# Variance of rows: TensorE's row sums replaced by passes on DVE and ACT, with a new assignment of rows to partitions

## The chip, the cores and the metric

The kernel runs on one core of a Trainium2 chip. The metric is the time of one execution on the device in microseconds (us), taken as the median of several runs. The engines named below are TensorE (PE, the matrix engine), VectorE (DVE), ScalarE (ACT), GpSimd (POOL) and SyncE (SP), which here only issues DMA transfers. The core has 16 DMA engines, which move data between HBM and the on-chip memory.

## The reference

```python
def setup_inputs():
    batch, seq, dim = 32, 512, 1024
    return {"x": np.random.randn(batch, seq, dim).astype(np.float32)}

def reference(x):
    mean_sq = np.mean(x**2, axis=-1)
    sq_mean = np.mean(x, axis=-1)**2
    return (mean_sq - sq_mean).astype(np.float32)
```

For each of 32 x 512 = 16384 rows of 1024 float32 values, the variance is wanted: 67.1 MB are read and 64 KB written.

## The kernel before

**Layout.** The rows are spread over 128 partitions, 128 rows in a row for each partition. "Column" c is the set of the c-th rows of all partitions, so a load of n columns (`col_range`) takes n x 4 KB of contiguous memory for each partition, and the pitch from partition to partition is 128 rows, 512 KB.

**Loads.** SP issues all loads, in this order: `xt_fill` (columns 120 to 127, L79), then 13 groups of 8 columns (`xt`, L165) in a pool of three buffers, then the end columns 104 to 119 into `xt_end` (L195) in loads of 4, 4, 2, 2, 2, 1 and 1 columns. The load of group g+3 waits until group g's buffer is free; the loads of `xt_end` and `xt_fill` have memory of their own.

**Work on a group.** Each row needs its mean and its mean square. There are three ways:

- `do_bn_col`: DVE takes statistics of two halves of 512 elements (L112) and aggregates them to mean and variance (L115). Columns 0 to 2 of a group.
- `do_square_col` on ACT (L118) gives the mean square of columns 3 to 7. The sum of columns 3 and 4 is a reduction on DVE (L171).
- The sum of columns 5 to 7: `do_tensor_cols` transposes and adds eight blocks of 128 x 128 on TensorE (L133), DVE copies the result to `folded` (L142), and TensorE multiplies by a column of ones (L143).

In groups 2 to 9 one column of `xt_fill` is done beside, by ACT and TensorE. `combine` turns sums and mean squares into variances with a short Square on ACT (L83) and a subtraction on DVE (L90, L102). ACT issues the store of columns 0 to 103 (L189).

**End.** The 16 columns of `xt_end` go by the pattern "CSAA": C is ACT's mean square with DVE's reduction (L206), S is two passes on ACT (L118 and L213), A is `do_bn_col`. After the last column a Square on ACT (L221), a subtraction on DVE (L230) and the store of columns 104 to 127 on SP (L237) follow.

**Order.** Each engine runs its own list of instructions in order, and semaphores hold an instruction until its inputs are there. The framework places the semaphores and may move an instruction a little within its engine's list.

Of the kernel before, what the change touches and what calls it, by code (L numbers as in the profile page):

```python
# [3 lines left out]

# [4 lines left out]


# [1 line left out]
def kernel(  # L13
# [2 lines left out]
    x: bass.AP,  # L16
    out: bass.AP,
):
    nc = tc.nc
    P = nc.NUM_PARTITIONS  # L20
    FP32 = mybir.dt.float32

    xf = x.flatten_outer_dims()
    N, D = xf.shape
    assert N % P == 0
    ntiles = N // P
    DCH = D // P

    def col_range(c0, n):
        return dataclasses.replace(  # L30
            xf,
            offset=c0 * D,
            ap=[[ntiles * D, P], [D, n], [1, D]],
        )

    out_ji = dataclasses.replace(out, offset=0, ap=[[ntiles, P], [1, ntiles]])

    FMAX = nc.vector.BN_STATS_FMAX
    nsub = (D + FMAX - 1) // FMAX

    inv_sqrt_d = 1.0 / math.sqrt(D)

    NBODY = 13
    END0 = NBODY * 8
    FILL0 = 120

    end_plan = [
        (104, 4),
        (108, 4),
        (112, 2),  # L50
        (114, 2),
        (116, 2),
        (118, 1),
        (119, 1),
    ]

    xpool = ctx.enter_context(tc.tile_pool(name="xpool", bufs=3))
    spool = ctx.enter_context(tc.tile_pool(name="spool", bufs=8))
    fpool = ctx.enter_context(tc.tile_pool(name="fpool", bufs=4))
    scpool = ctx.enter_context(tc.tile_pool(name="scpool", bufs=2))  # L60
    opool = ctx.enter_context(tc.tile_pool(name="opool", bufs=1))
    ppool = ctx.enter_context(tc.tile_pool(name="ppool", bufs=5, space=bass.MemoryType.PSUM))
    pspool = ctx.enter_context(tc.tile_pool(name="pspool", bufs=2, space=bass.MemoryType.PSUM))

    ident = opool.tile([P, P], FP32)
    masks.make_identity(nc, ident)
    ones = opool.tile([P, 1], FP32)
    nc.gpsimd.memset(ones, 1.0)

    pair_stage = opool.tile([P, 2, ntiles], FP32)  # L70
    msq_stage = opool.tile([P, ntiles], FP32)
    sqm_stage = opool.tile([P, ntiles], FP32)

    scratch = scpool.tile([P, D], mybir.dt.bfloat16)

    xt_end = opool.tile([P, FILL0 - END0, D], FP32)
    xt_fill = opool.tile([P, ntiles - FILL0, D], FP32)

    nc.sync.dma_start(out=xt_fill, in_=col_range(FILL0, ntiles - FILL0))  # L79

    def combine(c0, ngrp, gsize, nbn):
        n = ngrp * gsize
        nc.scalar.activation(  # L83
            out=sqm_stage[:, c0 : c0 + n],
            in_=pair_stage[:, 0, c0 : c0 + n],
            func=mybir.ActivationFunctionType.Square,
            scale=1.0 / D,
        )
        if nbn == 0:
            nc.vector.tensor_tensor(  # L90
                out=pair_stage[:, 1, c0 : c0 + n],
                in0=msq_stage[:, c0 : c0 + n],
                in1=sqm_stage[:, c0 : c0 + n],
                op=mybir.AluOpType.subtract,
            )
        else:
            var_v = pair_stage[:, 1, c0 : c0 + n].rearrange(
                "p (g k) -> p g k", k=gsize
            )
            msq_v = msq_stage[:, c0 : c0 + n].rearrange("p (g k) -> p g k", k=gsize)  # L100
            sqm_v = sqm_stage[:, c0 : c0 + n].rearrange("p (g k) -> p g k", k=gsize)
            nc.vector.tensor_tensor(  # L102
                out=var_v[:, :, nbn:gsize],
                in0=msq_v[:, :, nbn:gsize],
                in1=sqm_v[:, :, nbn:gsize],
                op=mybir.AluOpType.subtract,
            )

    def do_bn_col(xcol, i):
        stats = spool.tile([P, nsub, 6], FP32, name="stats")  # L110
        for s in range(nsub):
            nc.vector.bn_stats(  # L112
                out=stats[:, s, :], in_=xcol[:, s * FMAX : (s + 1) * FMAX]
            )
        nc.vector.bn_aggr(out=pair_stage[:, :, i], in_=stats)  # L115

    def do_square_col(xcol, i):
        nc.scalar.activation(  # L118
            out=scratch,
            in_=xcol,  # L120
            func=mybir.ActivationFunctionType.Square,
            scale=inv_sqrt_d,
            accum_out=msq_stage[:, i : i + 1],
        )

    def do_tensor_cols(xt, cols):
        if not cols:
            return
        psum_s = pspool.tile([P, 8], FP32, name="psum_s")
        for slot, (k, i) in enumerate(cols):  # L130
            psum_f = ppool.tile([P, P], FP32, name="psum_f")
            for ch in range(DCH):
                nc.tensor.matmul(  # L133
                    out=psum_f,
                    lhsT=xt[:, k, ch * P : (ch + 1) * P],
                    rhs=ident,
                    is_transpose=True,
                    start=(ch == 0),
                    stop=(ch == DCH - 1),
                )  # L140
            folded = fpool.tile([P, P], FP32, name="folded")
            nc.vector.tensor_copy(out=folded, in_=psum_f)  # L142
            nc.tensor.matmul(  # L143
                out=psum_s[:, slot : slot + 1],
                lhsT=folded,
                rhs=ones,
                start=True,
                stop=True,
            )
        i0 = cols[0][1]  # L150
        nt = len(cols)
        nc.vector.tensor_copy(  # L152
            out=pair_stage[:, 0, i0 : i0 + nt], in_=psum_s[:, :nt]
        )

    def do_filler_col(j):
        i = FILL0 + j
        do_square_col(xt_fill[:, j, :], i)
        do_tensor_cols(xt_fill, [(j, i)])

    for gi in range(NBODY):
        c0 = gi * 8
        nbn, ncl = 3, 2
        xt = xpool.tile([P, 8, D], FP32, name="xt")
        nc.sync.dma_start(out=xt, in_=col_range(c0, 8))  # L165

        for k in range(nbn):
            do_bn_col(xt[:, k, :], c0 + k)
        for k in range(nbn, 8):
            do_square_col(xt[:, k, :], c0 + k)  # L170
        nc.vector.reduce_sum(  # L171
            out=pair_stage[:, 0, c0 + nbn : c0 + nbn + ncl],
            in_=xt[:, nbn : nbn + ncl, :],
            axis=mybir.AxisListType.X,
        )
        do_tensor_cols(
            xt, [(k, c0 + k) for k in range(nbn + ncl, 8)]
        )

        if 2 <= gi <= 9:  # L180
            do_filler_col(gi - 2)

        if gi == 7:
            combine(0, 8, 8, 3)
        elif gi == 10:
            combine(120, 1, 8, 0)
        elif gi == 12:
            combine(64, 5, 8, 3)
            nc.scalar.dma_start(  # L189
                out=out_ji[:, 0:END0], in_=pair_stage[:, 1, 0:END0]  # L190
            )

    for (c0, ncols) in end_plan:
        off = c0 - END0
        nc.sync.dma_start(  # L195
            out=xt_end[:, off : off + ncols, :], in_=col_range(c0, ncols)
        )
        for k in range(ncols):
            i = c0 + k
            mode = "CSAA"[(i - END0) % 4]  # L200
            xcol = xt_end[:, off + k, :]
            if mode == "A":
                do_bn_col(xcol, i)
            elif mode == "C":
                do_square_col(xcol, i)
                nc.vector.reduce_sum(  # L206
                    out=pair_stage[:, 0, i : i + 1],
                    in_=xcol,
                    axis=mybir.AxisListType.X,
                )  # L210
            else:
                do_square_col(xcol, i)
                nc.scalar.activation(  # L213
                    out=scratch,
                    in_=xcol,
                    func=mybir.ActivationFunctionType.Copy,
                    accum_out=pair_stage[:, 0, i : i + 1],
                )

    n_end = ntiles - END0  # L220
    nc.scalar.activation(  # L221
        out=sqm_stage[:, END0:ntiles],
        in_=pair_stage[:, 0, END0:ntiles],
        func=mybir.ActivationFunctionType.Square,
        scale=1.0 / D,
    )
    var_v = pair_stage[:, 1, END0:ntiles].rearrange("p (g k) -> p g k", k=4)
    msq_v = msq_stage[:, END0:ntiles].rearrange("p (g k) -> p g k", k=4)
    sqm_v = sqm_stage[:, END0:ntiles].rearrange("p (g k) -> p g k", k=4)
    nc.vector.tensor_tensor(  # L230
        out=var_v[:, :, 0:2],
        in0=msq_v[:, :, 0:2],
        in1=sqm_v[:, :, 0:2],
        op=mybir.AluOpType.subtract,
    )

    nc.sync.dma_start(  # L237
        out=out_ji[:, END0:ntiles], in_=pair_stage[:, 1, END0:ntiles]
    )


# [28 lines left out]
```

## Time and profile before

| | us |
|---|---|
| median of 3 runs | 167.70 (167.53 to 167.71) |
| profiled execution, first to last instruction (span; the page gives no other time for it) | 165.9 |
| DVE busy | 107.0 |
| ACT busy | 99.7 |
| TensorE matmul busy | 82.8 |
| mean rate of the DMA engines over the span | 405 GB/s |

The span runs from the first to the last instruction on the core. "Busy" is time in which an engine executed an instruction. Busy shares are means over the whole span; which engine or transfer sets the end is read from the waits and from the windows of each stage. A line number in a profile is a line of the kernel that the profile belongs to.

### The profile page before, as it was taken

Reading aid. Unit: us, or ns where it says so; the run is one execution under the profiler, and the core shown is the slowest. Engines: PE = TensorE matmul, PEld = TensorE weight load, DVE = VectorE, ACT = ScalarE, POOL = GpSimd, SP = SyncE. Lnnn points to the kernel's source line nnn. Section 1 sums busy time; section 2 is a strip of 40 time slices with the busy share of each in tenths; the row PEclk is TensorE's granted clock in tenths of the full one; section 3 lists DMA queues with packets and bytes.
Section 4 is the critical chain, followed back from the end, with each engine's and each line's share of the span. In section 5 each row is a group of like instructions: output and inputs, shape, how many; then the busy total and the mean of one; then the engine's idle time right before and its main releaser. Section 6 shows DMA issues by size and latency. Waiting matters only on the chain.

```text
span 165.9 us, 1460 instructions
## 1 busy us (share of the span) xinstructions
PE 82.8 (50%) x470; PEld 78.6 (47%) x470; DVE 107.0 (64%) x230; ACT 99.7 (60%) x175; POOL 0.7 (0%) x7
## 2 busy tenths in 40 slices
PE   0000047293791957749497774929565391950000
PEld 0000046292780947749396764829464381930000
DVE  0000049295791967949396794939769393999993
ACT  3000049093790967939396694939767391998981
POOL 1000000000000000000000000000000000000000
PEclk9999999658576597865858598795978658585555
DMA  5999999999999999999999999999999999999930
GB/s 190 443 427 450 411 450 411 443 443 427 450 399 450 421 435 435 421 443 411 443 423 443 427 435 435 419 450 415 435 435 419 443 421 399 435 417 417 412 140 3
DMA packets 3320, 67.26 MB, mean 405 GB/s; under 512 B 625, under 2 KB 625, under 8 KB 881
## 3 DMA queue, kind: packets, MB, share of 16 engines
q1 hardware_dynamic: 3168, 67.12, 94.7%
q8 instruction: 3, 0.05, 0.1%
q10 hardware_dynamic: 144, 0.05, 0.1%
q14 instruction: 5, 0.03, 0.1%
HBM read 67.11 MB, written 0.07 MB: 405 GB/s over the span
## 4 chain that ended last, share of the span: by engine, by line
DMA 69%; DVE 28%; issue 0%; SPq 0%; ACT 0%; ACTq 0%
DMA xt<-in_x_dram 69%; DVE stats L112 16%; DVE pair_stage L171 7%; DVE pair_stage L206 3%; DVE pair_stage L115 2%; DVE folded L142 0%; SPq L79 0%; ACT sqm_stage L221 0%; SPq L165 0%; DVE pair_stage L230 0%; DVE pair_stage L102 0%; DVE pair_stage L152 0%; ACTq L221 0%
## 5 line engine op out<-in xcount | busy, mean ns | idle before, releaser
L118 ACT ACTIVATE scratch<-xt 128x1024 bf16<-128x1024 f32 x65 | 68.7, 1057 | 59.6 <-DMA xt<-in_x_dram 57.9
L133 PE MATMUL psum_f<-ident,xt 128*128 128x128 f32 x312 | 62.9, 392 | 53.9 <-DMA xt<-in_x_dram 53.9
L133 PEld LDWEIGHTS psum_f<-ident,xt 128*128 128x128 f32 x312 | 59.1, 212 | 54.9 <-DMA xt<-in_x_dram 31.8
L112 DVE BATCH_NORM_STATS2 stats<-xt 128x6 f32<-128x512 f32 x78 | 48.8, 667 | 50.5 <-DMA xt<-in_x_dram 50.5
L171 DVE TENSOR_REDUCE pair_stage<-xt 128x2 f32<-128x2048 f32 x13 | 29.5, 2270 | 0.0
L143 PEld LDWEIGHTS psum_s<-ones,folded 128*128 128x128 f32 x94 | 11.5, 191 | 14.6 <-DVE folded L142 14.6
L143 PE MATMUL psum_s<-ones,folded 128*128 128x1 f32 x94 | 12.5, 252 | 11.4 <-DVE folded L142 11.4
L118 ACT ACTIVATION_READ_ACCUMULATOR scratch<-xt 128x1 f32 x65 | 12.1, 186 | 0.0
L112 DVE BATCH_NORM_STATS2 stats<-xt_end 128x6 f32<-128x512 f32 x16 | 10.1, 666 | 0.0
L142 DVE COPY folded<-psum_f 128x128 f32<-128x128 f32 x47 | 9.8, 267 | 0.0
L115 DVE BATCH_NORM_AGGREGATE pair_stage<-stats 128x2 f32<-128x12 f32 x47 | 9.2, 197 | 0.1
L118 ACT ACTIVATE scratch<-xt_end 128x1024 bf16<-128x1024 f32 x8 | 8.5, 1056 | 1.1 <-DMA xt_end<-in_x_dram 0.9
L133 PE MATMUL psum_f<-ident,xt_fill 128*128 128x128 f32 x64 | 9.0, 286 | 0.0
L118 ACT ACTIVATE scratch<-xt_fill 128x1024 bf16<-128x1024 f32 x8 | 8.5, 1057 | 0.3
L133 PEld LDWEIGHTS psum_f<-ident,xt_fill 128*128 128x128 f32 x64 | 8.2, 155 | 0.0
L152 DVE COPY pair_stage<-psum_s 128x3 f32<-128x3 f32 (+1 forms) x21 | 3.3, 159 | 5.2 <-PE psum_s L143 4.7
L206 DVE TENSOR_REDUCE pair_stage<-xt_end 128x1 f32<-128x1024 f32 x4 | 4.7, 1185 | 0.0
L213 ACT ACTIVATE scratch<-xt_end 128x1024 bf16<-128x1024 f32 x4 | 4.2, 1056 | 0.1
L118 ACT ACT_TABLE_LOAD x1 | 1.3, 1283 | 0.7 <-PEq L254 0.7
L118 ACT ACTIVATION_READ_ACCUMULATOR scratch<-xt_end 128x1 f32 x8 | 1.5, 186 | 0.0
L118 ACT ACTIVATION_READ_ACCUMULATOR scratch<-xt_fill 128x1 f32 x8 | 1.5, 186 | 0.0
L83 ACT ACTIVATE sqm_stage<-pair_stage 128x64 f32<-128x64 f32 (+2 forms) x3 | 0.7, 228 | 0.7 <-DVE pair_stage L152 0.7
(12 smaller groups left out, 2.7 us busy)
## 6 DMA issues: line engine op xcount, KB each, us to landing
xt<-in_x_dram SPq DMA_DIRECT2D x13, 4096.0 KB, 23.1
xt_fill<-in_x_dram SPq DMA_DIRECT2D x1, 4096.0 KB, 12.6
xt_end<-in_x_dram SPq DMA_DIRECT2D x2, 2048.0 KB, 29.8
xt_end<-in_x_dram SPq DMA_DIRECT2D x3, 1024.0 KB, 36.1
xt_end<-in_x_dram SPq DMA_DIRECT2D x2, 512.0 KB, 24.1
out_dram<-pair_stage ACTq DMA_DIRECT2D x1, 52.0 KB, 6.8
out_dram<-pair_stage SPq DMA_DIRECT2D x1, 12.0 KB, 1.4
```

The lines of the kernel that those rows point to most:

```text
L83: nc.scalar.activation(out=sqm_stage[:, c0 : c0 + n], in_=pair_stage[:, 0, c0 : c0 + n], func=mybir.ActivationFunctionType.Square, scale=1 ...
L112: nc.vector.bn_stats(out=stats[:, s, :], in_=xcol[:, s * FMAX : (s + 1) * FMAX])
L115: nc.vector.bn_aggr(out=pair_stage[:, :, i], in_=stats)
L118: nc.scalar.activation(out=scratch, in_=xcol, func=mybir.ActivationFunctionType.Square, scale=inv_sqrt_d, accum_out=msq_stage[:, i : i + 1],)
L133: nc.tensor.matmul(out=psum_f, lhsT=xt[:, k, ch * P : (ch + 1) * P], rhs=ident, is_transpose=True, start=(ch == 0), stop=(ch == DCH - 1),)
L142: nc.vector.tensor_copy(out=folded, in_=psum_f)
L143: nc.tensor.matmul(out=psum_s[:, slot : slot + 1], lhsT=folded, rhs=ones, start=True, stop=True,)
L152: nc.vector.tensor_copy(out=pair_stage[:, 0, i0 : i0 + nt], in_=psum_s[:, :nt])
L171: nc.vector.reduce_sum(out=pair_stage[:, 0, c0 + nbn : c0 + nbn + ncl], in_=xt[:, nbn : nbn + ncl, :], axis=mybir.AxisListType.X,)
L206: nc.vector.reduce_sum(out=pair_stage[:, 0, i : i + 1], in_=xcol, axis=mybir.AxisListType.X,)
L213: nc.scalar.activation(out=scratch, in_=xcol, func=mybir.ActivationFunctionType.Copy, accum_out=pair_stage[:, 0, i : i + 1],)
```

## The change

TensorE, GpSimd's constants, PSUM and the short subtractions at the end are no longer used. Every column is done by one engine alone: DVE by statistics and aggregation as before, ACT by a Copy pass that gives the negative mean (scaled by the root of 1/D) and a Square pass with that as its bias, whose accumulated output is the variance. In a group of 8, ACT takes columns 0, 3 and 6 and DVE the other five; ACT does its three Copy passes first and then its three Square passes.

There is no `xt_fill`. The 13 groups come first; 24 end columns follow in loads of 7, 5, 4, 2, 2, 1 and 1 columns, and columns 126 and 127 in two halves of 512 elements each, taken by DVE half by half. The first 127 columns have 127 rows in a row per partition (pitch 508 KB), and column 127 is the last 128 rows of the input, one per partition. Two stores end the kernel: ACT stores columns 0 to 126 (508 bytes per partition) once column 126 is done, and SP stores column 127 (4 bytes per partition).

```diff
-    def col_range(c0, n):
-        return dataclasses.replace(
-            xf, offset=c0 * D, ap=[[ntiles * D, P], [D, n], [1, D]],
-        )
+    MAIN = ncols - 1
+    def load(dst, c0, n, f0=0, f=D):
+        if c0 == MAIN:
+            offset, ap = MAIN * P * D, [[D, P], [1, f]]
+        else:
+            offset, ap = c0 * D, [[MAIN * D, P], [D, n], [1, f]]
+            if n == 1:
+                ap = [[MAIN * D, P], [1, f]]
+        nc.sync.dma_start(
+            out=dst, in_=dataclasses.replace(xf, offset=offset + f0, ap=ap)
+        )
...
-    end_plan = [(104, 4), (108, 4), (112, 2), (114, 2), (116, 2), (118, 1), (119, 1)]
+    END_LOADS = [7, 5, 4, 2, 2, 1, 1]
+    END_WHO = "ADDADDADADDADADDADDADA"
...
-    nc.sync.dma_start(out=xt_fill, in_=col_range(FILL0, ntiles - FILL0))
...
+    def dve_col(xcol, c):
+        stats = spool.tile([P, 2, 6], FP32, name="stats")
+        dve_half(stats, 0, xcol[:, :H])     # bn_stats
+        dve_half(stats, 1, xcol[:, H:])     # bn_stats
+        dve_done(stats, c)                  # bn_aggr into mv[:, :, c]
+
+    def act_cols(cols):
+        s = D ** -0.5
+        for xcol, c in cols:
+            nc.scalar.activation(out=junk, in_=xcol, func=ACTF.Copy,
+                scale=-s / D, accum_out=neg_mean[:, c : c + 1])
+        for xcol, c in cols:
+            nc.scalar.activation(out=junk, in_=xcol, func=ACTF.Square,
+                scale=s, bias=neg_mean[:, c : c + 1],
+                accum_out=mv[:, 1, c : c + 1])
...
+    for g in range(NGROUPS):
+        c0 = g * GROUP
+        xt = xpool.tile([P, GROUP, D], FP32, name="xt")
+        load(xt, c0, GROUP)
+        act_cols([(xt[:, k, :], c0 + k) for k in (0, 3, 6)])
+        for k in (1, 2, 4, 5, 7):
+            dve_col(xt[:, k, :], c0 + k)
...
+    for j in range(k, ncols - END0):
+        stats = spool.tile([P, 2, 6], FP32, name="stats")
+        for h in range(2):
+            xh = xt_end[:, j, h * H : (h + 1) * H]
+            load(xh, END0 + j, 1, h * H, H)
+            dve_half(stats, h, xh)
+        dve_done(stats, END0 + j)
+        if END0 + j == MAIN - 1:
+            nc.scalar.dma_start(
+                out=dataclasses.replace(out, offset=0, ap=[[MAIN, P], [1, MAIN]]),
+                in_=mv[:, 1, :MAIN],
+            )
+    nc.sync.dma_start(
+        out=dataclasses.replace(out, offset=MAIN * P, ap=[[1, P], [1, 1]]),
+        in_=mv[:, 1, MAIN:],
+    )
```

More of the change, by code (lines that the diff above doesn't have):

```diff
@@ L2 @@
 import dataclasses
-import math
 from contextlib import ExitStack
@@ L7 @@
 import concourse.tile as tile
-from concourse import bass_utils, masks, mybir
+from concourse import mybir
 from concourse._compat import with_exitstack
@@ L21 @@
     FP32 = mybir.dt.float32
+    ACTF = mybir.ActivationFunctionType
     xf = x.flatten_outer_dims()
@@ L25 @@
     assert N % P == 0
-    ntiles = N // P
-    DCH = D // P
-    def col_range(c0, n):
-        return dataclasses.replace(
-            xf,
-            offset=c0 * D,
-            ap=[[ntiles * D, P], [D, n], [1, D]],
-        )
[L36 to L55, printed above, removed]
+    ncols = N // P
@@ new lines @@
+    H = D // 2
+    MAIN = ncols - 1
[8 more added lines that the diff above has]
+            out=dst, in_=dataclasses.replace(xf, offset=offset + f0, ap=ap)
+        )
+    GROUP = 8
+    NGROUPS = 13
+    END0 = GROUP * NGROUPS
+    END_LOADS = [7, 5, 4, 2, 2, 1, 1]
@@ L57 @@
+    END_WHO = "ADDADDADADDADADDADDADA"
     xpool = ctx.enter_context(tc.tile_pool(name="xpool", bufs=3))
     spool = ctx.enter_context(tc.tile_pool(name="spool", bufs=8))
-    fpool = ctx.enter_context(tc.tile_pool(name="fpool", bufs=4))
-    scpool = ctx.enter_context(tc.tile_pool(name="scpool", bufs=2))
     opool = ctx.enter_context(tc.tile_pool(name="opool", bufs=1))
-    ppool = ctx.enter_context(tc.tile_pool(name="ppool", bufs=5, space=bass.MemoryType.PSUM))
-    pspool = ctx.enter_context(tc.tile_pool(name="pspool", bufs=2, space=bass.MemoryType.PSUM))
@@ L65 @@
[L65 to L77, printed above, removed]
-    nc.sync.dma_start(out=xt_fill, in_=col_range(FILL0, ntiles - FILL0))
@@ L81, in combine @@
[L81 to L87, printed above, removed]
-        )
[L89 to L94, printed above, removed]
-            )
-        else:
-            var_v = pair_stage[:, 1, c0 : c0 + n].rearrange(
-                "p (g k) -> p g k", k=gsize
-            )
[L100 to L235, printed above, removed]
+    mv = opool.tile([P, 2, ncols], FP32)
@@ new lines, with dve_half, dve_done @@
+    neg_mean = opool.tile([P, ncols], FP32)
+    junk = opool.tile([P, D], mybir.dt.bfloat16)
+    xt_end = opool.tile([P, ncols - END0, D], FP32)
+    def dve_half(stats, h, xh):
+        nc.vector.bn_stats(out=stats[:, h, :], in_=xh)
+    def dve_done(stats, c):
+        nc.vector.bn_aggr(out=mv[:, :, c], in_=stats)
+    def dve_col(xcol, c):
[3 more added lines that the diff above has]
+        dve_done(stats, c)
@@ new lines, in act_cols @@
+    def act_cols(cols):
+        s = D ** -0.5
+        for xcol, c in cols:
+            nc.scalar.activation(
+                out=junk,
+                in_=xcol,
+                func=ACTF.Copy,
+                scale=-s / D,
+                accum_out=neg_mean[:, c : c + 1],
+            )
+        for xcol, c in cols:
+            nc.scalar.activation(
+                out=junk,
+                in_=xcol,
+                func=ACTF.Square,
+                scale=s,
+                bias=neg_mean[:, c : c + 1],
+                accum_out=mv[:, 1, c : c + 1],
+            )
@@ new lines @@
+    for g in range(NGROUPS):
[5 more added lines that the diff above has]
+            dve_col(xt[:, k, :], c0 + k)
+    k = 0
+    for n in END_LOADS:
+        load(xt_end[:, k : k + n, :] if n > 1 else xt_end[:, k, :], END0 + k, n)
+        act_cols(
+            [
+                (xt_end[:, j, :], END0 + j)
+                for j in range(k, k + n)
+                if END_WHO[j] == "A"
+            ]
+        )
+        for j in range(k, k + n):
+            if END_WHO[j] == "D":
+                dve_col(xt_end[:, j, :], END0 + j)
+        k += n
@@ L237 @@
+    for j in range(k, ncols - END0):
[9 more added lines that the diff above has]
+                in_=mv[:, 1, :MAIN],
+            )
     nc.sync.dma_start(
-        out=out_ji[:, END0:ntiles], in_=pair_stage[:, 1, END0:ntiles]
+        out=dataclasses.replace(out, offset=MAIN * P, ap=[[1, P], [1, 1]]),
+        in_=mv[:, 1, MAIN:],
```

## The prediction

> **What bounds the kernel now.** I read the page's slices and queue table first, then the chain of waits in order of time, the windows by stage, and last the timeline of the end.
>
> ```profile
> span 165.9 us, 1460 instructions
> ...
> DMA  5999999999999999999999999999999999999930
> ...
> q8 instruction: 3, 0.05, 0.1%
> ...
> q14 instruction: 5, 0.03, 0.1%
> ```
>
> All 16 DMA engines are busy from the second slice to the 38th. So loading is the bound, and an engine matters only where it delays a load or stands behind the last one. The chain of waits gives the pace (start, duration, what):
>
> ```profile
> 29.19 24.30 DMA xt<-in_x_dram
> 53.51 1.88 DVE stats L112 x3
> ...
> 59.63 22.99 DMA xt<-in_x_dram
> 82.64 1.88 DVE stats L112 x3
> ...
> 88.77 23.06 DMA xt<-in_x_dram
> 111.86 1.88 DVE stats L112 x3
> ...
> 117.98 23.04 DMA xt<-in_x_dram
> 141.05 1.88 DVE stats L112 x3
> ```
>
> Work on groups 0, 3, 6, 9 and 12 starts at 23.05 (not shown), 53.51, 82.64, 111.86 and 141.05: three loads of 4 MB take 30.46, 29.13, 29.22 and 29.19 us, so 9.72 us each, with one loss of about 1.3 us before 53.51. The trace's packet records explain it: the packets of 32 KB take 1.213 to 1.22 us nearly throughout, but a 16 KB packet of q8 at 49.08 held one DMA engine for 1.10 us and the load packet after it took 1.68. The loads land with their slowest engine: from the landing counts, the first and last of the 16 are 0.73 us apart for the first four loads and 2.05 to 2.19 us apart from the fifth on. The windows show it at the end (columns: length, five engines, clock, DMA share, GB/s):
>
> ```profile
> 150.90:156.00 5.10, 0.00 (x0) 0.00 (x0) 5.07 (x9) 4.97 (x9) 0.00 (x0) 0.50 1.01 419
> ...
> 158.00:159.00 1.00, 0.00 (x0) 0.00 (x0) 0.96 (x4) 0.52 (x1) 0.00 (x0) 0.50 0.64 254
> 159.00:160.00 1.00, 0.00 (x0) 0.00 (x0) 1.00 (x2) 0.97 (x3) 0.00 (x0) 0.50 0.30 119
> 160.00:161.00 1.00, 0.00 (x0) 0.00 (x0) 1.00 (x3) 0.97 (x3) 0.00 (x0) 0.50 0.08 33
> ```
>
> Most engines are done by 159; a share of 0.30 is about five engines still at work, and the last ends near 160.9. Then comes the tail:
>
> ```profile
> 160.84 1.06 ACT L213 ACTIVATE scratch<-xt_end 128x1024 bf16<-128x1024 f32 x1
> ...
> 161.41 0.21 DVE L115 BATCH_NORM_AGGREGATE pair_stage<-stats 128x2 f32<-128x12 f32 x1
> 161.53 1.23 DVE L112 BATCH_NORM_STATS2 stats<-xt_end 128x6 f32<-128x512 f32 x2
> 162.80 0.21 DVE L115 BATCH_NORM_AGGREGATE pair_stage<-stats 128x2 f32<-128x12 f32 x1
> 163.11 0.22 ACT L221 ACTIVATE sqm_stage<-pair_stage 128x24 f32<-128x24 f32 x1 [1.12 <-DVE pair_stage L115]
> 163.36 0.17 DVE L230 TENSOR_TENSOR pair_stage<-msq_stage,sqm_stage 128x12 f32<-128x12 f32 x1 [0.35 <-ACT sqm_stage L221]
> 163.56 0.35 SPq L237 DMA_DIRECT2D out_dram<-pair_stage  x1
> ```
>
> The last load lands at T = 160.9, DVE takes it up only at 161.53, and the store is issued at 163.56, which is T + 2.7. The store lands after 1.4 us and the span ends at 165.9, 2.3 after its issue. The page gives no time for its execution but the span; the median, 167.7, lies 1.8 above, and I add 1.8 to every span.
>
> **The body of the change.** TensorE's 940 instructions, DVE's 47 copies of `folded` (9.8 us), its 13 reductions (29.5 us) and the subtractions go. DVE gets 5 columns in 8. From 23.05 to 26.85 it did three columns in 3.80 us, so 1.27 a column and 6.3 us a group. ACT gets 3 columns at two passes; its starts stand 1.18 us apart (23.05, 24.23, 25.41), so 6 x 1.18 = 7.1 us. Both fit into 9.72, so this work is hidden and the removed work is worth nothing in the body; the cover fails only if ACT's group went beyond 9.72, or 1.62 a pass. The load of group g+3 waits for the buffer of group g, now 7.1 us after landing instead of 6.0; SP has queued behind it only loads. At that point 2.6 us of group g+1 and 9.72 of g+2 are still queued, against a start-up of some 1.4 us (the share of 0.55 in the first 3 us). No bubble.
>
> **The loads.** The bytes are equal. `xt_fill`'s 4 MB no longer go first, so the engines begin 9.7 us sooner, and the end has 24 columns instead of 16: seven loads and four halves. Packet records: 32 KB 1.213 us, 16 KB 0.612, 8 KB 0.311, 4 KB 0.159; the last two give 0.007 us fixed per packet, so 2 KB should take 0.083. Eight packets per engine and load: 7 columns 8.5 us, 5 columns 6.1, 4 columns 4.9, 2 and 2 5.0, 1 and 1 2.55, four halves 2.66, sum 29.7. Before, the same 24 columns took 9.7 for `xt_fill` plus 19.8 (141.05 to 160.9, 16 columns in seven loads), 29.5 to 29.6. Cost: +0.1. From the other side, if 2 KB packets took as long as 4 KB ones, +2.4 more.
>
> The Trainium skill, "DMA: Bandwidth & Descriptors", section "Anatomy of one DMA", speaks against small loads: it fits a fixed 2.0 us to a DMA issued from GpSimd; two more loads would by that make it 4 us worse. The seven loads in 19.8 us show no such cost once several are queued; I keep +0.1.
>
> SP must still issue them in time. Before, SP waited three times (20.1 us in total) at L195 for landings of earlier loads: the landing counts use eight counters, so each DMA waits for the one eight before. After, the last half waits for the first 2-column load, which lands at T - 7.7; that is early enough. Behind it on SP stands only the last store.
>
> The pitch between partitions becomes 127 rows (508 KB) instead of 128. With the packets at a flat 1.213 us I see nothing to gain; what is above the flat (up to 1.22 later on) is at most 0.8 us over the run. A loss can't be excluded and is the slower rival.
>
> The same page, section "Latency and other measured facts", has 207 GB/s in each direction at a pitch of 512 KiB where 214 is full; by that the loads' 157 us would shrink by 5. The flat packets at the old pitch speak against that here, and I take 0.
>
> **The instruction packets.** q8's three packets (49.08, 83.14, 115.97) come 34.1 and 32.8 us apart; by the windows TensorE and its loads run some 80 instructions in 9.8 us, so about 270 between two packets. I take q8 to be TensorE's, and it goes. But q14 has 8 KB packets at 57.19, 67.15 and 135.85 too, each beside a load packet that took 1.59 to 1.88. In the landing counts one DMA engine that was 1.1 us behind before 135.85 is 2.06 behind after, almost as late as the three that q8 hit (up to 2.18). DVE runs 15 instructions a group against 14 to 17 before, ACT 12 against 10 to 13, so q14's packets stay. Gain: 0.1 if two still fall on one engine, about 1.1 if they fall on different ones. I take 0.1, by the row that shows it happening. With +0.1 for the small loads T stays at 160.9.
>
> **The tail.** With the landings at T - 21.2, -15.1, -10.2, -7.7, -5.2, -4.0, -2.7 and halves at -2.0, -1.3, -0.7 and 0, DVE (1.27 a column) finishes column 124 at about T - 2.5 and then waits for the halves. ACT (2.36 a column) stays behind from the 7-column load on: 3 columns to T - 14.1, then -9.4, -7.0, -4.6, -2.3 and, for column 125, T + 0.1. A Square now reads the sum that the Copy before it left; between nothing and 0.2 each (0.22 is a whole short activation, L221), so ACT ends between T + 0.1 and T + 1.1. I take T + 0.3, since the 1.18 spacing already holds the read of the accumulator.
>
> DVE after T: the aggregate of column 126 may stand behind the first half of 127 (the chain shows three statistics before each aggregate), 0.1; statistics 0.67; gap 0.04; aggregate 0.21; 0.03 to the issue. Sum T + 1.05, against T + 2.7: 1.65 saved. What goes is the 0.7 of backlog, one half's statistics, L221 and L230.
>
> The two stores: ACT's 65 KB go out at about T + 0.4 into empty queues and land, like the last store did after 1.4, near T + 1.9; the store before that took 6.8 us did so among loads. The last store has 4 bytes a partition; the nearest rows are the old one (96 bytes, 1.4 us) and the 4-byte counts in the packet records (9 ns each). I take 1.4, with 0 to +0.6 for the range. It is issued at T + 1.05 and is the last: 160.9 + 1.05 + 2.3 = 164.25 of span, 1.6 less than 165.9. Time: 164.25 + 1.8 = 166.0.
>
> **The rivals.** (a) The slow DMA engines disappear with TensorE's instruction packets: T falls by about 1.1, and so does the time, to 164.9. For it: three of the four latest engines are q8's. Against: the fourth is q14's.
>
> (b) The tail shrinks less: DVE's aggregate waits for ACT's writes to `mv`, or the ACT store is late and lands last. If DVE's column 127 were held until ACT ends (T + 0.3 to T + 1.1), its two halves, the aggregate and the gaps (1.6) put the store at T + 1.9 to T + 2.7: 166.9 to 167.7, in the middle 167.3. Against: the aggregate at 150.69 wrote `pair_stage` while ACT's store from it, issued at 150.20, was in flight for 6.8 us, so neighbouring columns don't hold each other up.
>
> (c) Slower: the new pitch makes loads slower all along. It decides from 0.10 us per 4 MB on, which over 16 loads eats the 1.6. The slowest window of a whole load (131.20 to 141.05) moved 415 GB/s against 427 for the mean pace to 141.05; that rate throughout would add 4.5 us, so 170.5. Nothing in the profile asks for it.
>
> (d) The change does nothing: were the work off the critical path in the tail too, 167.7. The timeline of the tail excludes most of this.
>
> **How the numbers follow.** Forecast 166.0 with 0.51 (own range 165.4 to 166.6); (a) 0.27 (164.5 to 165.4); (b) 0.10 (166.8 to 167.7); (c) 0.09 (168.1 to 170.5); (d) 0.03. The range 164.5 to 167.4 leaves out (c), (d) and a little of (b). About 0.2% (0.3 us) is what a measurement here can tell from no change: faster 0.87, same 0.04, slower 0.09.
>
> **What would show it.** Right: body landings 9.7 us apart; no q8 packets; the last store issued about 1.0 us after the last landing; span near 164.2. Spread of DMA share over the last 2 us: still 2 us for the forecast, about 1 for (a). Wrong: groups landing 9.8 or more apart (c), or DVE idle after T waiting for ACT (b).

## The result and the profile after

The changed kernel takes 173.33 us (172.52 to 174.22, 4 runs) against 167.69: slower, ratio 1.0339 (95% interval 1.0303 to 1.0374). The profiled execution took 173.12 us for a span of 171.3, so again 1.8 lie around the span. The forecast was 166.0.

From the page of the changed kernel's profile, the lines that answer to those of before:

```profile
span 171.3 us, 535 instructions
...
DMA  7999999999999999999999999999999999999000
...
q14 instruction: 4, 0.03, 0.0%
```

q8 is gone with TensorE, q14 is still there, and the DMA engines end one slice earlier relative to the span than before: three slices, some 13 us, hold no loads to speak of. The chain of waits (start, duration, what) gives the pace of the loads:

```profile
13.11 1.16 ACT junk L77 x2
...
42.30 1.16 ACT junk L77 x2
...
71.83 1.16 ACT junk L77 x2
...
100.97 1.16 ACT junk L77 x2
```

Work on groups 0, 3, 6 and 9 starts 29.19, 29.53 and 29.14 us apart, 9.7 us a group as before and as forecast. So the body is untouched. The windows at the end (columns: length, DVE, ACT, POOL, clock, DMA share, GB/s):

```profile
158.00:159.00 1.00, 0.83 (x3) 1.00 (x2) 0.00 (x0) 1.00 0.58 213
159.00:160.00 1.00, 1.00 (x2) 0.97 (x3) 0.00 (x0) 1.00 0.10 39
160.00:161.00 1.00, 0.97 (x4) 0.97 (x3) 0.00 (x0) 1.00 0.01 4
161.00:162.00 1.00, 0.68 (x2) 0.63 (x2) 0.00 (x0) 1.00 0.00 0
162.00:163.00 1.00, 0.00 (x0) 0.00 (x0) 0.00 (x0) 1.00 0.30 66
163.00:171.30 8.30, 0.00 (x0) 0.00 (x0) 0.00 (x0) 1.00 0.00 0
```

The loads are done before 161: by the landing counts (each DMA leaves 16 counts in the trace, and it has landed with the last of them) at 160.62. The stores' packets run between 162 and 163, and then nothing at all is busy for 8 us, neither an engine nor a DMA engine. The timeline and the table of DMA issues (the last column is the time from issue to landing) say what is waited for:

```profile
160.23 1.23 DVE L62 BATCH_NORM_STATS2 stats<-xt_end 128x6 f32<-128x512 f32 x2
160.39 1.15 ACT L85 ACTIVATE junk<-xt_end,neg_mean 128x1024 bf16<-128x1024 f32 x1
161.45 0.19 ACT L85 ACTIVATION_READ_ACCUMULATOR junk<-xt_end,neg_mean 128x1 f32 x1
161.50 0.21 DVE L65 BATCH_NORM_AGGREGATE mv<-stats 128x2 f32<-128x12 f32 x1
161.66 0.40 ACTq L124 DMA_DIRECT2D out_dram<-mv  x1
161.74 0.35 SPq L129 DMA_DIRECT2D out_dram<-mv  x1
```

```profile
out_dram<-mv ACTq DMA_DIRECT2D x1, 63.5 KB, 7.9
out_dram<-mv SPq DMA_DIRECT2D x1, 0.5 KB, 8.7
```

The last store is issued at 161.74, 1.8 us earlier than before (163.56). But it lands 8.7 us after its issue instead of 1.4, and the store beside it is as late, 7.9 us. The packet records make it odder: each of the 4-byte packets took 7 to 9 ns and the last of them began at 162.97; the landings came between 165.1 and 170.4. The 7.3 us between 8.7 and 1.4 are the whole difference to the forecast. The question for the runs: which store is slow, and why.

### The profile page after: what moved, and what is told of

It reads as the page before. It is cut to its first block, busy times and chain, and to the rows that moved or that the text cites. A ratio compares the mean times of both kernels' runs of the same rounds, so it can differ in the third digit from the quotient of the medians.

```text
span 171.3 us, 535 instructions
## 1 busy us (share of the span) xinstructions
DVE 105.0 (61%) x240; ACT 116.0 (68%) x193; POOL 0.2 (0%) x4
## 4 chain that ended last, share of the span: by engine, by line
DMA 75%; ACT 17%; DVE 2%; issue 1%; ACTq 0%
DMA xt<-in_x_dram 59%; DMA xt_end<-in_x_dram 16%; ACT junk L85 9%; ACT junk L77 8%; DVE stats L62 1%; DVE mv L65 0%; ACTq L77 0%
## 5 line engine op out<-in xcount | busy, mean ns | idle before, releaser
L62 DVE BATCH_NORM_STATS2 stats<-xt 128x6 f32<-128x512 f32 x130 | 80.8, 663 | 52.3 <-DMA xt<-in_x_dram 52.3
L77 ACT ACTIVATE junk<-xt 128x1024 bf16<-128x1024 f32 x39 | 41.2, 1057 | 41.9 <-DMA xt<-in_x_dram 41.1
L85 ACT ACTIVATE junk<-xt,neg_mean 128x1024 bf16<-128x1024 f32 x39 | 44.8, 1148 | 1.3
L62 DVE BATCH_NORM_STATS2 stats<-xt_end 128x6 f32<-128x512 f32 x30 | 18.7, 666 | 3.7 <-DMA xt_end<-in_x_dram 3.6
L65 DVE BATCH_NORM_AGGREGATE mv<-stats 128x2 f32<-128x12 f32 x80 | 15.8, 198 | 0.7
L85 ACT ACTIVATE junk<-xt_end,neg_mean 128x1024 bf16<-128x1024 f32 x9 | 10.3, 1147 | 0.3
L77 ACT ACTIVATE junk<-xt_end 128x1024 bf16<-128x1024 f32 x9 | 9.5, 1056 | 1.4 <-DMA xt_end<-in_x_dram 1.2
L85 ACT ACTIVATION_READ_ACCUMULATOR junk<-xt,neg_mean 128x1 f32 x39 | 7.3, 187 | 0.0
L77 ACT ACTIVATION_READ_ACCUMULATOR junk<-xt 128x1 f32 x39 | 7.3, 186 | 0.0
L85 ACT ACTIVATION_READ_ACCUMULATOR junk<-xt_end,neg_mean 128x1 f32 x9 | 1.7, 186 | 0.0
```

The source lines that it names most:

```text
L62: nc.vector.bn_stats(out=stats[:, h, :], in_=xh)
L65: nc.vector.bn_aggr(out=mv[:, :, c], in_=stats)
L77: nc.scalar.activation(out=junk, in_=xcol, func=ACTF.Copy, scale=-s / D, accum_out=neg_mean[:, c : c + 1],)
L85: nc.scalar.activation(out=junk, in_=xcol, func=ACTF.Square, scale=s, bias=neg_mean[:, c : c + 1], accum_out=mv[:, 1, c : c + 1],)
```

## The experiments

**Which of the two stores.** Theory A blames the 4-byte store, theory B the 508-byte pieces that touch each other, theory C that both are in flight together. First, the changed kernel without the 4-byte store:

```diff
-    nc.sync.dma_start(out=dataclasses.replace(out, offset=MAIN * P, ap=[[1, P], [1, 1]]),
-                      in_=mv[:, 1, MAIN:])
```

> The changed kernel without SP's store of column 127 (4 bytes per partition); those 128 results are left out. Theory A: ACT's store lands 1.5 to 2 us after its issue, time 165.5 to 166.3. Theory B: it still takes about 8 us, time 172 to 173. Theory C: as A, 165.5 to 166.3.

And the changed kernel without the 508-byte store:

```diff
-        if END0 + j == MAIN - 1:
-            nc.scalar.dma_start(out=..., in_=mv[:, 1, :MAIN])
```

> The changed kernel without ACT's store of columns 0 to 126 (508 bytes per partition); those results are left out. Theory A: SP's 4-byte store still takes 7 to 8 us, time 172 to 173. Theory B: it lands after 1.4 us, time 165.5 to 166.3. Theory C: as B, 165.5 to 166.3.

Measured: 166.02 us without the 4-byte store (165.92 to 166.18; ratio to the kernel before 0.9904, interval 0.9889 to 0.9919), and 172.21 without the 508-byte store (171.91 to 172.33; ratio 1.0270, 1.0254 to 1.0285). The issue rows of the two runs, in this order:

```profile
out_dram<-mv ACTq DMA_DIRECT2D x1, 63.5 KB, 1.7
```

```profile
out_dram<-mv SPq DMA_DIRECT2D x1, 0.5 KB, 7.8
```

64 KB in 508-byte pieces land after 1.7 us, half a KB in 4-byte pieces after 7.8. Theory A holds. The 508-byte store is late only beside the other: 7.9 with it, 1.7 without it. What the two together add (theory C) is small, some 1 us: 173.3 with both, 172.2 with the slow one alone.

**The stores by themselves.** Ten forms of stores, one after the other:

> No variance is computed: the kernel only stores tiles of 128 partitions to the output, one store after the other has landed, in ten forms named by bytes per partition and pitch in bytes (s508p508 is the changed kernel's first store, s4p4 its second, s96p512 the last store of the kernel before), each form twice. Theory A (many 4-byte writes into the same few hundred bytes wait for each other): s4p4 takes 7 to 8 us from issue to landing, s508p508 1.4 to 2. Theory B (508-byte pieces whose ends share a stretch of memory with the next partition's piece wait for each other): s508p508 takes 7 to 8 us, s4p4 1.4 to 2, and s508p512, whose pieces do not touch, 1.4 to 2. Theory C (only the two stores together are slow): every form 1.4 to 2 us.

Timeline of that run, the instruction that waits for each landing (in brackets how long it waited); the four rows belong to s508p508, s4p4, s508p512 and s4p512:

```profile
6.92 0.17 DVE L51 MEMSET s508p<- 128x128 f32 x1 [1.85 <-DMA out_dram<-s508p]
15.33 0.17 DVE L51 MEMSET s4p<- 128x128 f32 x1 [7.98 <-DMA out_dram<-s4p]
17.58 0.17 DVE L51 MEMSET s508p<- 128x128 f32 x1 [1.82 <-DMA out_dram<-s508p]
19.59 0.17 DVE L51 MEMSET s4p<- 128x128 f32 x1 [1.59 <-DMA out_dram<-s4p]
```

With no other transfer in flight, 4 bytes per partition at a pitch of 4 took 7.8 and 7.2 us from issue to landing, and the same 4 bytes at a pitch of 512 took 1.4, as quick as any other form (1.4 to 1.8 us; one of four 508-byte stores, at a pitch of 512, took 2.4). So small pieces alone are not slow, and neither are pieces that touch, such as the 508 bytes at a pitch of 508 (1.7 and 1.8). Slow are 128 pieces of 4 bytes side by side.

**How near is too near.** The same with other sizes and pitches:

> No variance is computed: stores alone as before, each after the last has landed, each form twice, named by bytes per partition and pitch in bytes (s32p32o16: 32 bytes that begin 16 bytes off a multiple of 32). If writes that share a stretch of 64 bytes go one after another, some 0.4 us each: s4p4 7.5 us, s4p8 and s8p8 4.2, s4p16 and s16p16 2.6, s4p32 1.8, s4p64 1.4. If the stretch is 32 bytes, some 0.9 us each: s4p4 7.5, s4p8 and s8p8 4, s4p16 and s16p16 2.3, s4p32 and s4p64 1.4. If it is 512 bytes, 0.05 each: s4p4 7.5, s4p8 4.5, s4p16 3, s4p32 2.2, s4p64 1.8.

Issue rows (names ending in x are of the first round of the forms, in y of the second):

```profile
out_dram<-s4p64x SPq DMA_DIRECT2D x1, 0.5 KB, 1.5
out_dram<-s8p8x SPq DMA_DIRECT2D x1, 1.0 KB, 3.2
out_dram<-s16p16x SPq DMA_DIRECT2D x1, 2.0 KB, 1.4
...
out_dram<-s4p4y SPq DMA_DIRECT2D x1, 0.5 KB, 7.2
out_dram<-s4p8y SPq DMA_DIRECT2D x1, 0.5 KB, 2.9
out_dram<-s4p16y SPq DMA_DIRECT2D x1, 0.5 KB, 1.4
out_dram<-s4p32y SPq DMA_DIRECT2D x1, 0.5 KB, 1.7
```

Pitch 4 is slow (7.2 and 7.7), pitch 8 much less so (2.9 to 3.2, with 4 or 8 bytes), and from 16 on it is over, within 1.4 to 1.9. None of the three expected tables fits: with stretches of 64 or 32 bytes, pitch 16 should have cost 2.3 to 2.6, with stretches of 512 bytes 3. A guess was left: from 128 partitions four neighbours may go through one DMA engine, so that at pitch 16 each 64 bytes belong to one engine. Stores from 16 partitions test it:

> No variance is computed: stores of 4 bytes per partition alone, each after the last has landed, each form twice, from 16 partitions (n16) or 128 (n128), at pitches of 4 to 64 bytes. The stores so far were slow at pitches 4 and 8 and quick from 16 on. Theory E (what costs is that different DMA engines write into the same 64 bytes; four neighbouring partitions go through one engine when there are 128, and each of 16 partitions goes through an engine of its own): n16s4p4 5 to 8 us, n16s4p16 clearly above 1.6 (2.5 to 4), n16s4p64 1.4, n128s4p16 1.4. Rival H (what costs is that the written addresses lie less than 16 bytes apart, whichever engine writes): n16s4p16 1.4, n16s4p4 and n16s4p8 slow. Rival I (only the number of writes counts): n16s4p4 2 us or less.

```profile
out_dram<-n16s4p4x SPq DMA_DIRECT2D x1, 0.1 KB, 1.3
...
out_dram<-n128s4p4x SPq DMA_DIRECT2D x1, 0.5 KB, 7.6
out_dram<-n128s4p16x SPq DMA_DIRECT2D x1, 0.5 KB, 1.4
```

From 16 partitions every pitch took 1.3 us (one reading of 2.2 at pitch 8), even the 64 bytes that all 16 write into; from 128, 7.6 and 7.2 at pitch 4 and 1.4 at pitch 16. In the packet records up to six packets of that first store run at the same time, which speaks for several DMA engines at work in its 64 bytes, as theory E has it. So theory E falls, rival H falls with it, and rival I can't explain why 128 writes at pitch 16 are quick. One more run looked at the growth:

> No variance is computed: stores of 4 bytes per partition alone, each after the last has landed, each form twice, from 32, 64, 96 or 128 partitions at pitches of 4, 8 or 12 bytes. From 16 partitions at pitch 4 the store took 1.3 us, from 128 7.2 to 7.8. Theory J (each write waits for the other writes to its 64 bytes, so the price grows with the writes that a DMA engine has in such stretches): n32s4p4 about 2.2, n64s4p4 about 4, n96s4p4 about 5.8, n64s4p8 about 2.1, n128s4p12 between 1.4 and 2.9. Rival K (a threshold: only a full 128 is slow): n32s4p4, n64s4p4 and n96s4p4 1.3 to 1.5.

```profile
out_dram<-n32s4p4x SPq DMA_DIRECT2D x1, 0.1 KB, 3.4
out_dram<-n64s4p4x SPq DMA_DIRECT2D x1, 0.2 KB, 7.7
out_dram<-n96s4p4x SPq DMA_DIRECT2D x1, 0.4 KB, 6.8
out_dram<-n64s4p8x SPq DMA_DIRECT2D x1, 0.2 KB, 3.6
out_dram<-n128s4p12x SPq DMA_DIRECT2D x1, 0.5 KB, 2.4
```

At pitch 4 it grows from 1.3 (16 partitions) over 3.4 and 3.8 (32) to 6.2 to 7.8 (64 and more) and stays there. That is neither in proportion to the writes (theory J) nor a threshold at 128 (rival K). The law behind it stays open; the price of the form that the kernel uses is measured.

**Hiding it under the loads.** If the store is only slow to land, it should cost nothing early in the kernel. Column 127 goes first:

```diff
+    xt_last = opool.tile([P, D], FP32)
+    load(xt_last, MAIN, 1)
+    dve_col(xt_last, MAIN)
+    nc.scalar.dma_start(out=dataclasses.replace(out, offset=MAIN * P, ap=[[1, P], [1, 1]]),
+                        in_=mv[:, 1, MAIN:])
...
-    nc.sync.dma_start(out=dataclasses.replace(out, offset=MAIN * P, ap=[[1, P], [1, 1]]), ...)
```

> The changed kernel with its layout and both its stores, but column 127 is loaded and worked on first, and its 4-byte store is issued by ACT at the start; the 508-byte store of the other 127 columns is the last. If the 4-byte store costs only because it stands at the end: it still takes 7 to 8 us, beside the loads, and the time is 165.7 to 166.6. If slow writes hold up the loads on the same DMA engines as well: 168 or more.

Measured 172.97 us (172.26 to 173.39; ratio 1.0309, 1.0279 to 1.0339), about as slow as at the end. One window of the changed kernel (columns as above), and the same window and the issue row of this one:

```profile
12.80:25.60 12.80, 9.31 (x21) 9.82 (x17) 0.00 (x0) 1.00 0.98 422
```

```profile
12.80:25.60 12.80, 6.53 (x15) 7.17 (x12) 0.00 (x0) 1.00 0.89 243
```

```profile
out_dram<-mv ACTq DMA_DIRECT2D x1, 0.5 KB, 19.1
```

Among the loads the store takes 19.1 us, and in those 12.8 us the loads get 243 GB/s instead of 422. By the landing counts the last load comes at 166.05 instead of 160.62, 5.4 later. The packet records tie the two together: the store's packets begin between 9.49 and 24.47, in this stretch load packets of 32 KB take up to 3.74 us, and right after it, from 26 on, 1.2 again. So the slow writes hold up the loads on the DMA engines, and at this place the loads don't hide them. A smaller part of the time has another reason: the last store now waits for ACT and is issued 2.4 us after the last landing (168.41) instead of 1.1. It lands after 1.6.

**The change without the new assignment of rows.** The changed kernel with 128 rows per partition and, in place of its two stores, one of 512 bytes per partition:

```diff
-    MAIN = ncols - 1
+    MAIN = ncols
...
+    nc.sync.dma_start(out=dataclasses.replace(out, offset=0, ap=[[ncols, P], [1, ncols]]),
+                      in_=mv[:, 1, :])
```

> The changed kernel with the old assignment of rows (128 rows in a row per partition, pitch 512 KB) and one store of 512 bytes per partition by SP at the end. Theories A, B and C: the store lands after 1.4 to 1.6 us, the last load at 160.5 to 161, time 165.5 to 166.5. Rival D (something else in the changed end, such as the halves, is slow as well): over 167.

166.20 us (166.10 to 166.64), ratio 0.9921 (0.9904 to 0.9939): 0.8% faster than the kernel before. The last load lands at 160.82, the store is issued at 161.96 and lands after 1.6. Rival D falls. So without the new assignment of rows and its 4-byte store the change gives the 166.0 that was forecast, and the pitch of 127 rows neither gives nor takes anything visible in the loads (160.62 against 160.82).

**The late DMA engine.** In these runs the last of the 16 landing counts of a load is still 2.0 us behind the first at the end. In the changed kernel this spread goes from 0.71 to 1.09 with the fifth load, after an 8 KB packet of q14 at 43.62, and from 1.09 to 2.05 with the 13th, after another at 127.12, when DVE had started 50 and 182 instructions. With the 13th load the last but one count is only 0.76 behind the first, so the second packet hit the engine that was the latest already. Theory F takes both packets for DVE's instructions. The first test leaves out DVE's aggregations in the groups:

```diff
         for k in (1, 2, 4, 5, 7):
-            dve_col(xt[:, k, :], c0 + k)     # two bn_stats, one bn_aggr
+            dve_stats(xt[:, k, :])           # two bn_stats
```

> The kernel with 128 rows per partition and one store, without the 65 aggregations of the groups (their results are left out): DVE has 176 instructions instead of 240. Theory F (DVE's second 8 KB instruction packet, at 127 us after its 182nd instruction, falls on the DMA engine that the first one fell on, and makes it 2.0 us late instead of 1.1): that packet comes after the last load or not at all, the last load lands 0.9 to 1.0 us earlier, near 159.9, time 165.1 to 165.4. Rival G (the late DMA engine is late for another reason): 166.0 to 166.4 as without the edit.

The second keeps all results and does the aggregation of all 65 columns at once (ACT takes columns 0 to 2 of a group here instead of 0, 3 and 6):

```diff
+    gstats = opool.tile([P, 5 * NGROUPS, 4, 3], FP32)   # (count, mean, M2) of quarters
...
+    combine_groups()    # M2 and squared means summed, minus the square of the mean
```

> The kernel with 128 rows per partition and one store; the 65 aggregations of the groups are replaced by five instructions after the last group, so DVE has 180 instructions. All results are computed. Theory F: as in the run without the aggregations, 165.1 to 165.5, unless the packet comes just before the end. Rival G: 166.0 to 166.4. If the five instructions delay the end columns on DVE: the store is issued later than 1.1 us after the last landing.

165.70 us (165.51 to 165.83; ratio 0.9881, 0.9864 to 0.9897) and 165.80 (165.62 to 166.14; ratio 0.9888, 0.9873 to 0.9903). The packet at 127 is gone in both, the last load lands at 160.24 and 160.26, and the engines end 1.4 to 1.5 us apart. So the second packet was DVE's, and it made the last load late, but by less than theory F has it: by 0.6 of the 0.9 to 1.0 expected: q14's packet at 149.0, when ACT had started 190 instructions, now makes another engine the latest (without the aggregations, the spread goes from 1.16 to 1.63 with the next load). The times lie between the ranges of theory F and rival G. The gain over the 128-row kernel, 0.4 to 0.5 us, is about as large as that kernel's scatter; the landings carry the reading. The kernel with one combination is the fastest that computes every result: 1.1% faster than before, 4.3% faster than the change.

## Why the prediction was wrong, step by step

**The step that failed** is the sentence on the last store: "The last store has 4 bytes a partition; the nearest rows are the old one (96 bytes, 1.4 us) and the 4-byte counts in the packet records (9 ns each). I take 1.4, with 0 to +0.6 for the range." It measured 8.7 us (7.8 without the other store). That is 7.3 more, and 166.0 + 7.3 = 173.3 is the measured time. Both rows were near in size and far in what counts: the old store's pieces stood 512 bytes apart, and the form with 96 bytes at that pitch took 1.4 us alone as well; no row of the old profile had 128 pieces of 4 bytes at a pitch of 4. The packet time was also the wrong measure: the 4-byte packets took 7 to 9 ns here too, and the last count landed 7.4 us after the last of them began. What makes the writes slow stays open. No rival priced this; the slower one, (c), was about the pitch of the loads, and the pitch cost nothing.

**Right by its own terms:**

- The body: 9.7 us a load, ACT's group of work 7.3 us (13.11 to 20.45 in the chain) against 7.1, hidden as forecast, and TensorE's removal worth nothing in it.
- The loads: the last 24 columns took 29.62 us (131.00 to 160.62) against 29.7. The last load landed at 160.6 against T = 160.9.
- The instruction packets: q8 went and q14 stayed. That two of DVE's fall on one DMA engine was the forecast's choice against rival (a), and it is what the landings show (0.71, 1.09, 2.05). The forecast left out one more 8 KB packet of q14 before, at 159.50; its like in the changed kernel, at 149.37, did not hit the latest engine. The Trainium skill, "Runtime: NRT & Kernel Launch", section "Instruction fetch mechanics", has an engine fetch its instructions by a DMA queue of its own and calls the cost mostly hidden. The packets are seen here, TensorE's on q8, DVE's and ACT's both under q14. For these loads the cost is not all hidden: a packet sets back one DMA engine, the load waits for the latest, and without DVE's second packet the last load landed 0.6 us earlier.
- The tail up to the issue: T + 1.12 against T + 1.05. DVE's part came within 0.1 of what was worked out.

**Wrong without effect:** The end has three more loads than before (eleven instead of eight), not two, so the 4 us that spoke against small loads should have been 6; the 29.62 us show none of them. With eight counters the last half waits for the 4-column load, not for the first 2-column one; that load landed at 150.51, and SP issued the half at 150.53, ten us before it landed.

**Mis-sized without effect on the last store's issue:** ACT was to end at T + 0.3, in bounds of 0.1 to 1.1, and ended at 161.64, T + 1.0. The groups of the changed kernel show why:

```profile
L77 ACT ACTIVATE junk<-xt_end 128x1024 bf16<-128x1024 f32 x9 | 9.5, 1056 | 1.4 <-DMA xt_end<-in_x_dram 1.2
...
L85 ACT ACTIVATE junk<-xt_end,neg_mean 128x1024 bf16<-128x1024 f32 x9 | 10.3, 1147 | 0.3
```

The pass whose bias is a column of a tile takes 0.09 us more than the Copy. ACT is behind all through the end, so nine of these add up to 0.8. (The forecast's upper bound had no full sum behind it: 0.2 for each of nine Squares would be T + 1.9.) The 0.09 is also what the Trainium skill states ("ScalarE: Activation LUTs", section "What ACT_TABLE_LOAD costs": some 93 ns for a pointer operand); it would have sized the term. DVE ends at 161.71, after ACT, so SP's store was not issued later for it. ACT's store came to stand beside SP's; whether an earlier one would have saved some of the 1 us that the two cost together, no run shows.

## What to carry to other kernels

Price a store by the number and pitch of its pieces at the destination, not by its bytes alone, and by issue to landing, not by its packets' time: 128 partitions writing 4 bytes side by side took 7 to 8 us where 4 bytes at a pitch of 16 or more, or 512 bytes each, took 1.4 to 1.7. A layout that leaves one column over is paid for in such a store, and moving it under the loads at the start only moved the price here (172.97 us against 173.33). In a kernel bound by its loads, the landing counts of each load tell how far the latest DMA engine is behind and since when; an 8 KB instruction packet put the latest one 0.4 to 1.0 us further back here.

## What the runs showed that was not expected

A store of 512 bytes in all took the loads of the whole core down to 243 GB/s for some 13 us and itself landed after 19.1 us. The price of 4-byte pieces at pitch 4 goes from 1.3 us for 16 partitions to 3.4 to 3.8 for 32 and 6.2 to 7.8 for 64 and more; what makes it so stays open. Stores whose 508-byte or 448-byte pieces touch each other (1.5 to 1.8 us) are as quick as those of 508 or 512 bytes at a pitch of 512 (1.5 to 1.7, one reading 2.4).
